# Two encoder layers on one core: products of the merge gates move one stage ahead, and the recurrence works in strips of 32 keys

## The chip, the cores and the metric

The kernel runs on one core of one Trainium2 chip. The metric is the device time of one execution in microseconds; of several runs the median is taken.

## The reference

A batch of one sequence of 512 tokens with 1024 features goes through two layers, in fp32. `w_in` (1024 features in, 8608 out) is one projection whose output is cut into the inputs of three mixers and three gates; each mixer's output is projected, weighted by the sigmoid of its gate and summed:

```python
for l in range(DEPTH):                                  # DEPTH = 2
    h = _rmsnorm(x, g_mix[l])
    (a_cq, a_ckv, a_kr, b_q, b_ff, b_fb, b_i, b_g,
     c_q, c_k, c_v, gate_a, gate_b, gate_c) = _split_cols(h @ w_in[l], IN_SPLITS)
    y_a = _mla(a_cq, a_ckv, a_kr, ...)                   # latent attention
    y_b = _hgrn2(b_q, b_ff, b_fb, b_i, b_g, ...)         # gated linear recurrence, both directions
    y_c = _window_gqa(c_q, c_k, c_v, ...)                # windowed attention
    merged = (jax.nn.sigmoid(gate_a) * (y_a @ w_br_a[l])
              + jax.nn.sigmoid(gate_b) * (y_b @ w_br_b[l])
              + jax.nn.sigmoid(gate_c) * (y_c @ w_br_c[l]))
    x = x + merged @ w_out[l]
    x = x + _cross(_rmsnorm(x, g_x[l]), _rmsnorm(mem, g_mem[l]), ...)
    x = x + _swiglu(_rmsnorm(x, g_ffn[l]), ...)
return _rmsnorm(x, g_final)
```

The recurrence has 8 heads with keys of 128 and values of 64 features. For each of its two directions a state `S_t = diag(f_t) S_(t-1) + k_t v_t^T` is read by `q_t`; the reference computes it in chunks of 16 tokens. Since `f` only decays, the sum over both directions can be written as one matrix of scores over all 512 x 512 pairs of tokens, times the values.

## The kernel before

Activations lie feature by feature: a tile has 128 features (or tokens of keys) on its partitions and the 512 tokens along its free axis. A product on TensorE takes a weight block of 128x128 (or smaller) and moves up to 512 columns through it into a bank of PSUM; there are eight banks, handed out in turn.

**Weights.** Every weight is streamed from DRAM in units of four blocks (256 KB, tile `wraw`), in the order in which the program asks for them. `_next` (by way of `_fetch`, L112) keeps the fetches up to five units ahead, on SP's queue. `_part` makes two tiles of a unit, up to three units ahead: `whi` is the value rounded to fp32r (ScalarE, L120), `wlo` what the rounding left (VectorE, L121). With activations split the same way (`split`, L180 on ScalarE, L181 on VectorE), `mm3` makes one fp32-like block product of three fp32r products. A projection of 1024 features into 128 is eight blocks, two units, 24 products. All matmuls are issued from one line, L151.

**Order.** The text of the program gives what each engine is to do; a scheduler may take instructions of one engine in another order where nothing forbids it, and each engine then runs its own list in order. Bars to free reordering are the rotating buffers: 25 tiles of 256 KB (`t2`), 14 large ones (`c8`), the eight banks, five units of weights.

**Stages of a layer.** Recurrence (`hgrn`), latent attention (`mla`), windowed attention (`window`), then output projection, cross attention and feed-forward part. `fillers` is a list of pieces of other work; `fill` takes the next piece at marked places of the attention stages. In the kernel before, `branch` makes these pieces: for two columns of blocks at a time it issues two gate projections, their sigmoids (L519), and two output projections of the mixer, each multiplied by its gate and added into `merged`. The pieces of mixer B fill the `mla` stage, those of A the `window` stage, those of C, but for a first gate, come behind it.

**Recurrence.** For each head `take_z` makes sigmoids of the two forget projections (L307, L308) and `hgrn_decay` (L394 on), for each direction, makes log decays, scans them (L411), and writes queries and keys scaled by decays: `qk` (tile `c`, keys at L439) for the pairs inside a strip of 32 tokens, and `lf`, `lr` (tile `c`, L457, on POOL and VectorE) for pairs of strips at four distances. `hgrn_scores` (L460 on) then makes the matrix of scores of a head. For each of four groups `j` of 128 tokens it takes `bd` and `bb`, the full 128x128 squares of both directions, of which only the four 32x32 blocks on the diagonal are kept by a mask (L482); neighbouring strips and halves are separate products of 32x32 and 64x64 that write over their parts of `bd`. Pairs of tokens in different groups are eight wide products into three further banks `g`. The result is split (L487, L488, and `split`) into `ah` and `al`; `vturn` turns the values so that keys lie on partitions, and splits them too. The value product of a head is twelve fp32r products into one bank, half of whose rows are that head's and are copied out (L369).

The loop over heads `i` is written so that scores of head `i`, projections of head `i + 2` (`take_z`, `take_q`), the value product of head `i` and the decay of head `i + 2` follow each other; every second head (odd `i`) adds a gate of the recurrence itself (`g`), a sum over features and the normed output `y`.

Of the kernel before, what the change touches and what calls it, by code (L numbers as in the profile page):

```python
# [48 lines left out]
def _consts():  # L49
# [21 lines left out]
    mb = same & (p[:, None] >= p[None, :])  # L71
# [4 lines left out]
class _K:  # L76
# [119 lines left out]
    def setup(self):  # L196
# [25 lines left out]
        self.zz = self.tl("zz", [P, 2, 4, P])  # L222
        nc.gpsimd.memset(self.zz, 0.0)
# [66 lines left out]
    def hgrn(self, l, x, xg, acc):  # L290
# [13 lines left out]
        def take_z(hd, zs):  # L304
# [27 lines left out]
        take_z(heads[1], [proj("f", 1), proj("b", 1)])  # L332
# [3 lines left out]
        a = self.hgrn_scores(heads[0])  # L336
        decay(heads[1])
        y = self.pairs4(4)
        for i in range(8):
            pr = i // 2  # L340
            if i > 0:
                a = self.hgrn_scores(heads[i])
            if i % 2 == 0:
                osb = self.t2()
                if 0 < i < 6:
                    values(pr + 1)
            else:
# [6 lines left out]
            if i < 6:  # L354
                take_z(heads[i + 2], [proj("f", i + 2), proj("b", i + 2)])
# [7 lines left out]
            ob = self.bank()  # L363
            vh, vl = vs[pr]
# [95 lines left out]
    def hgrn_scores(self, hd):  # L460
# [5 lines left out]
        bd, bb = self.bank([P, 4, P]), self.bank([P, 4, P])  # L466
# [12 lines left out]
        ah, al = self.c8([P, 4 * T], F32R), self.c8([P, 4 * T], F32R)  # L479
        z = self.zz  # L480
        for i, b in enumerate((bd, bb)):
            nc.vector.copy_predicated(z[:, i], self.msk[:, i].unsqueeze(1).to_broadcast([P, 4, P]), b)  # L482
        zd = self.t2(shape=(P, 4, P))
        tt(zd, z[:, 0], z[:, 1], op=ALU.add)
        dg = lambda a: bass.AP(a.tensor, a.offset, [list(a.ap[0]), [640, 4], [1, P]])
        dh, dl = dg(ah), dg(al)
        nc.scalar.activation(dh, zd, AF.Copy)  # L487
        tt(dl, zd, dh.bitcast(F32), op=ALU.subtract)  # L488
        h0, h1 = slice(0, P), slice(P, 2 * P)
        for i in range(3):  # L490
# [12 lines left out]
            s = slice(i * 640 + 128, (i + 1) * 640)  # L503
            self.split(ah[:, s], al[:, s], g)
        return ah, al

    def branch(self, l, gate, wname, rows, y, h, merged, first):

        nc = self.nc
        allr = np.arange(D)  # L510
        st = {}

        def gates(c):
# [648 lines left out]
```

## Time and profile before

| | |
|---|---|
| median of 3 runs | 2450.2 us (2447.57 to 2451.07) |
| profiled execution, its own time | 2445.72 us |
| its span, first to last instruction | 2443.9 us |
| mean granted clock of TensorE | 0.994 |
| TensorE matmuls | 2396.9 us, 98% |
| VectorE | 1503.9 us, 62% |
| ScalarE | 1194.2 us, 49% |
| GpSimd | 262.9 us, 11% |
| DMA, mean | 90 GB/s, 29.8% of 16 engines |

The share of an engine is its busy time over the span; matmuls overlap, so a busy TensorE need not be at its peak. The granted clock is a share of 2.4 GHz: 1.00 is 2.4 GHz, 0.50 is 1.2 GHz. The list of waits says on what an engine that stood idle was waiting, and its sum is time lost only on the engine that sets the end. In windows each engine is given as busy time and the number of instructions under way in that stretch.

### The profile page before, as it was taken

The numbers are of one execution on the slowest core, as the hardware profiler recorded it, in microseconds if no ns is written. First come the engines' busy times: TensorE is split into PE (matmuls) and PEld (weight loads), VectorE is DVE, ScalarE is ACT, GpSimd is POOL, SyncE is SP. The second block draws the span as 40 slices with busy tenths as digits, with TensorE's granted clock in tenths as the row PEclk, the third lists the DMA queues.
The fourth block names the chain that finished last, engine by engine and source line by source line (L and its number), as shares of the span: only waits on it lengthen the run. The fifth ranks groups of instructions, "written<-read, shape, count | busy, mean of one in ns | idle before, by whom it ended". The sixth has DMA issues, their size and how long they took to land.

```text
span 2443.9 us, 32499 instructions
## 1 busy us (share of the span) xinstructions
PE 2396.9 (98%) x11974; PEld 1966.2 (80%) x11974; DVE 1503.9 (62%) x2745; ACT 1194.2 (49%) x2169; POOL 262.9 (11%) x197
## 2 busy tenths in 40 slices
PE   8999999999999999999998999999999999999998
PEld 6788877788888888888877887877888888888886
DVE  8877766665565655355577786666656566553553
ACT  7666665555444533233466665654544444332332
POOL 2455300000000000000035452000000000000000
PEclk9999999999999999999999999999999999999999
DMA  4212222123442333333421212212324522333332
GB/s 141 61 57 70 82 70 66 62 82 107 151 139 86 91 96 95 99 95 99 127 77 61 70 61 74 74 57 71 90 84 148 147 87 82 96 95 99 96 98 75
DMA packets 119681, 220.96 MB, mean 90 GB/s; under 512 B 13281, under 2 KB 15585, under 8 KB 119137
## 3 DMA queue, kind: packets, MB, share of 16 engines
q1 hardware_dynamic: 119520, 218.88, 29.8%
q8 instruction: 94, 1.54, 0.3%
q14 instruction: 67, 0.54, 0.1%
HBM read 214.63 MB, written 4.19 MB: 90 GB/s over the span
## 4 chain that ended last, share of the span: by engine, by line
PE 85%; DVE 8%; ACT 3%; POOL 2%; issue 1%; DMA 1%; SPq 0%; DVEq 0%; ACTq 0%; POOLq 0%
PE ps L151 83%; POOL t L404 2%; DVE c L457 1%; PE ps L643 1%; DVE smx L411 1%; PE ps L784 1%; POOL t L408 1%; DVE c L439 1%; DVE t L411 1%; DVE wlo L121 1%; DVE c L181 0%; ACT whi L120 0%; DVE c L438 0%; DVE zz L482 0%; DMA c<-in_memT_dram 0%
## 5 line engine op out<-in xcount | busy, mean ns | idle before, releaser
L151 PE MATMUL ps<-c,whi 128*128 128x512 f32 (+1 forms) x5696 | 1734.7, 387 | 6.5 <-ACT whi L120 6.2
L151 PEld LDWEIGHTS ps<-c,whi 128*128 128x128 f32 x5696 | 1059.4, 188 | 232.8 <-issue 10.4
L151 PE MATMUL ps<-c,wlo 128*128 128x512 f32 (+1 forms) x2848 | 1098.4, 386 | 15.3 <-DVE wlo L121 15.2
L120 ACT ACTIVATE whi<-wraw 128x512 fp32r<-128x512 f32 x764 | 475.3, 630 | 858.1 <-PE ps L151 626.3
L121 DVE TENSOR_TENSOR wlo<-wraw,whi 128x512 fp32r<-128x512 f32 x764 | 521.0, 690 | 552.9 <-ACT whi L120 539.8
L151 PEld LDWEIGHTS ps<-c,wlo 128*128 128x128 f32 x2848 | 536.1, 188 | 127.3 <-DVE wlo L121 20.5
L151 PE MATMUL ps<-c,t 128*128 128x512 f32 (+6 forms) x1024 | 188.0, 393 | 4.0 <-DVE c L181 3.7
L404 POOL TENSOR_SCALAR t<-t 128x512 f32<-128x512 f32 x32 | 71.8, 2244 | 1067.4 <-ACT t L401 1065.9
L151 PEld LDWEIGHTS ps<-c,t 128*128 128x128 f32 (+2 forms) x1024 | 127.8, 176 | 48.0 <-issue 20.2
L457 POOL TENSOR_TENSOR c<-c,smx 128x256 f32<-128x256 f32 x128 | 144.9, 1161 | 73.8 <-DVE c L438 61.4
L982 DVE TENSOR_TENSOR t<-ps,t 128x512 f32<-128x512 f32 x112 | 76.3, 688 | 103.0 <-PE ps L151 103.0
L151 PE MATMUL ps<-c 128*32 128x32 f32 (+3 forms) x1280 | 110.6, 259 | 5.5 <-DVE c L439 5.5
L151 PEld LDWEIGHTS ps<-c 128*32 128x32 f32 (+2 forms) x1280 | 96.8, 151 | 21.9 <-DVE c L439 4.0
L181 DVE TENSOR_TENSOR c<-ps,c 128x512 fp32r<-128x512 f32 (+2 forms) x126 | 80.2, 650 | 23.7 <-ACT c L180 23.4
L180 ACT ACTIVATE c<-ps 128x512 fp32r<-128x512 f32 (+2 forms) x126 | 68.4, 565 | 43.9 <-PE ps L151 42.6
L964 DVE TENSOR_TENSOR c<-ps,c 128x512 f32<-128x512 f32 x64 | 44.2, 691 | 72.8 <-PE ps L151 72.8
L457 DVE TENSOR_TENSOR c<-c,smx 128x256 f32<-128x256 f32 x128 | 67.7, 587 | 0.3
L408 POOL TENSOR_TENSOR t<-t,t 128x512 f32<-128x512 f32 x32 | 45.1, 1409 | 86.7 <-ACT t L407 86.7
L181 DVE TENSOR_TENSOR c<-t,c 128x512 fp32r<-128x512 f32 (+1 forms) x84 | 51.9, 632 | 2.9 <-ACT c L180 2.9
L180 ACT ACTIVATE c<-t 128x512 fp32r<-128x512 f32 (+1 forms) x84 | 48.0, 581 | 9.7 <-DVE t L390 3.3
L406 ACT ACTIVATE t<-t 128x512 f32<-128x512 f32 x32 | 20.1, 630 | 62.5 <-POOL t L404 62.5
L411 DVE TENSOR_TENSOR_SCAN t<-cst,t 128x512 f32<-128x512 f32 x32 | 40.8, 1275 | 15.8 <-POOL t L408 15.8
(145 smaller groups left out, 1830.6 us busy)
## 6 DMA issues: line engine op xcount, KB each, us to landing
wraw<-in_w_dram SPq DMA_DIRECT2D x764, 256.0 KB, 2.6
c<-in_xT_dram SPq DMA_DIRECT2D x16, 256.0 KB, 5.2
t<-in_bias_dram SPq DMA_DIRECT2D x16, 192.0 KB, 3.0
c<-in_memT_dram SPq DMA_DIRECT2D x3, 1024.0 KB, 8.1
xs<-c SPq DMA_DIRECT2D x8, 256.0 KB, 2.4
c<-xs SPq DMA_DIRECT2D x8, 256.0 KB, 5.3
out_dram<-t SPq DMA_DIRECT2D x8, 256.0 KB, 2.1
t<-in_rope_dram SPq DMA_DIRECT2D x4, 256.0 KB, 3.4
```

Source lines behind the costliest of these rows:

```text
L120: self.nc.scalar.activation(hi, raw, AF.Copy)
L121: self.nc.vector.tensor_tensor(lo, raw, hi.bitcast(F32), op=ALU.subtract)
L151: self.nc.tensor.matmul(o, a, b, start=start, stop=stop)
L180: nc.scalar.activation(hi, src, AF.Copy)
L181: nc.vector.tensor_tensor(lo, src, hi.bitcast(F32), op=ALU.subtract)
L404: nc.gpsimd.tensor_scalar(g, f, TINY, KNEE, op0=ALU.max, op1=ALU.min)
L408: nc.gpsimd.tensor_tensor(f, f, g, op=ALU.add)
L411: scan = lambda o, m, x: nc.vector.tensor_tensor_scan(o, m, x, 0.0, op0=ALU.mult, op1=ALU.add)
L439: nc.vector.scalar_tensor_tensor(ki, kk, omlb, cc, op0=ALU.mult, op1=ALU.mult)
L457: eng.tensor_tensor(ov, sv, ev, op=ALU.mult)
L964: nc.vector.tensor_tensor(x[c], b, xold[c], op=ALU.add)
L982: self.nc.vector.tensor_tensor(t, b, r, op=ALU.mult)
```

## The change

Three things change.

**Scores in strips.** For each group `j` the full squares are replaced by products of strips: four 32x32 on the diagonal of the forward direction (`bd`), four of the backward one (`bb`, now 32 columns wide), four of neighbouring strips, and four of 32 keys by 64 queries for the halves. Each sits on the 32 rows of PSUM of its strip. The wide products stay. The scores `a` are kept in one fp32 tile, not split in two: the predicated copies take the mask, ScalarE copies (`dg` and the three banks `g`), and four additions on 32 partitions bring in `bb`.

**Values of two heads at once.** `vturn` leaves the values in fp32. In odd iterations eight fp32 products, alternating between the two heads' halves of the rows, make the output of both heads in one bank, which is copied out once.

**Gates one stage ahead.** The gate projections of B are issued in the recurrence (two ahead of head 1's projections, then one in each of iterations 0 to 5), those of A in the `mla` stage, six of C in the `window` stage and two behind it. `gate_put` makes the sigmoid and writes it to DRAM; `out` reads it back ahead of its projection. The output projections stay where they were. This is 48 writes and 48 reads of 256 KB.

```diff
-        v = (self.t2(F32R, (P, 4, P)), self.t2(F32R, (P, 4, P)))
-        self.split(v[0], v[1], tb)
+        v = self.t2(shape=(P, 4, P))
+        nc.scalar.activation(v, tb, AF.Copy)
         return v
...
-        take_z(heads[1], [proj("f", 1), proj("b", 1)])
+        g0, g1, b0, b1 = self.projs("w_in", l, np.arange(D), [O_GB + ar, O_GB + P + ar, off["f"] + P + ar,
+                                                             off["b"] + P + ar], h)
+        take_z(heads[1], [b0, b1], [(0, g0), (1, g1)])
...
+            gs = [(i + 2, self.gate_proj(l, O_GB, i + 2, h))] if i < 6 else []
+            if i % 2 == 1:
                 g = proj("g", pr)
...
-                take_z(heads[i + 2], [proj("f", i + 2), proj("b", i + 2)])
+                take_z(heads[i + 2], [proj("f", i + 2), proj("b", i + 2)], gs)
...
-            for j in range(4):
-                s = slice(j * T, (j + 1) * T)
-                self.mm3(ob, (vh[:, j], vl[:, j]), (a[0][:, s], a[1][:, s]), j == 0, j == 3)
-            hf = slice(64 * (i % 2), 64 * (i % 2) + 64)
-            nc.scalar.activation(osb[hf], ob[hf], AF.Copy)
             if i % 2 == 1:
-                sq = self.t2()
+                ob = self.bank()
+                for j in range(4):
+                    for e in range(2):
+                        hf = slice(64 * e, 64 * e + 64)
+                        self.mm(ob[hf], vs[pr][:, j, hf], heads[i - 1 + e]["a"][:, j * T:(j + 1) * T], j == 0, j == 3)
+                osb, sq = self.t2(), self.t2()
+                nc.scalar.activation(osb, ob, AF.Copy)
...
-        for j in range(4):
-            js = slice(j * P, (j + 1) * P)
-            one(bd[:, j], qk[:, 1, js], qk[:, 0, js])
-            one(bb[:, j], qk[:, 3, js], qk[:, 2, js])
-        for j in range(4):
-            one(bd[0:64, j, 64:128], lf[:, 1, 1, 64 * j:64 * j + 64], lf[:, 1, 0, 64 * j:64 * j + 64])
-            one(bd[64:128, j, 0:64], lr[:, 1, 1, 64 * j:64 * j + 64], lr[:, 1, 0, 64 * j:64 * j + 64])
-            for i in range(2):
-                a, b = 64 * i, 64 * i + 32
-                ps = slice(64 * j + 32 * i, 64 * j + 32 * i + 32)
-                one(bd[a:a + 32, j, b:b + 32], lf[:, 0, 1, ps], lf[:, 0, 0, ps])
-                one(bd[b:b + 32, j, a:a + 32], lr[:, 0, 1, ps], lr[:, 0, 0, ps])
-        ah, al = self.c8([P, 4 * T], F32R), self.c8([P, 4 * T], F32R)
...
+        for j in range(4):
+            js = [slice(j * P + 32 * g, j * P + 32 * g + 32) for g in range(4)]
+            for g in range(4):
+                one(bd[q4[g], j, q4[g]], qk[:, 1, js[g]], qk[:, 0, js[g]])
+            for g in range(4):
+                one(bb[q4[g], j], qk[:, 3, js[g]], qk[:, 2, js[g]])
+            for g in range(4):
+                ps = slice(64 * j + 32 * (g // 2), 64 * j + 32 * (g // 2) + 32)
+                lt = lf if g % 2 == 0 else lr
+                one(bd[q4[g], j, q4[g ^ 1]], lt[:, 0, 1, ps], lt[:, 0, 0, ps])
+            for g in range(4):
+                ks = slice(64 * j + 32 * (g % 2), 64 * j + 32 * (g % 2) + 32)
+                lt = lf if g < 2 else lr
+                cs = slice(64, 128) if g < 2 else slice(0, 64)
+                one(bd[q4[g], j, cs], lt[:, 1, 1, ks], lt[:, 1, 0, 64 * j:64 * j + 64])
+        a = self.c8([P, 4 * T])
+        nc.vector.copy_predicated(self.zz, self.msk[:, 0].unsqueeze(1).to_broadcast([P, 4, P]), bd)
+        nc.vector.copy_predicated(self.zb, self.msk[:, 1, 0:32].unsqueeze(1).to_broadcast([P, 4, 32]), bb)
...
+        nc.scalar.activation(dg, self.zz, AF.Copy)
+        for g in range(4):
+            tt(dg[q4[g], :, q4[g]], self.zz[q4[g], :, q4[g]], self.zb[q4[g]], op=ALU.add)
...
-            self.split(ah[:, s], al[:, s], g)
-        return ah, al
+            nc.scalar.activation(a[:, i * 640 + 128:(i + 1) * 640], g, AF.Copy)
+        hd["a"] = a
...
+    def gate_put(self, sd, c, b):
+        sg = self.t2()
+        last = self.nc.scalar.activation(sg, b, AF.Sigmoid)
+        self.nc.sync.dma_start(sd[:, c], sg)
+        return last
...
+            def run():
+                sg = self.t2()
+                nc.sync.dma_start(sg, sd[:, c])
+                pb = self.projs(wname, l, rows, [c * P + np.arange(P)], y)[0]
...
-            self.fillers += self.branch(l, O_GB, "w_br_b", np.arange(512), yb, h, merged, True)
+            br = self.branch(l, sd, "w_br_b", np.arange(512), yb, merged, True)
+            sd, gs = self.gates(l, O_GA, h)
+            for c in range(0, KC, 2):
+                self.fillers += gs[c:c + 2] + [both(br[c], br[c + 1])]
...
-            self.fillers += self.branch(l, O_GA, "w_br_a", np.arange(512), ya, h, merged, False)
+            br = self.branch(l, sd, "w_br_a", np.arange(512), ya, merged, False)
+            sd, gs = self.gates(l, O_GC, h)
+            for c in range(6):
+                self.fillers += [gs[c], br[c]]
+            self.fillers += br[6:]
```

The mask `mb` becomes the triangle of a 32-wide strip, and `zz`, `zb` are the buffers that the predicated copies fill. The function `vtoken` of `mla` goes, since `vturn` now does the same.

On TensorE, at the scores of head 0 of layer 1, the kernel before had (`c_77` is `qk`, `c_81` is `lf`, `c_85` is `lr`, `ps_594` is `bd`, `ps_595` is `bb`):

```order
L151 MATMUL ps_594<-c_77_361 128x128
L151 MATMUL ps_595<-c_77_361 128x128
L151 MATMUL ps_594<-c_81_384 64x64
L151 MATMUL ps_594<-c_85_415 64x64
L151 MATMUL ps_594<-c_81_384 32x32
L151 MATMUL ps_594<-c_85_415 32x32
```

In the kernel after, the same place has (`ps_673` is `bd`, `ps_674` is `bb`):

```order
L151 MATMUL ps_673<-c_77_362 32x32 x4
L151 MATMUL ps_674<-c_77_362 32x32 x4
L151 MATMUL ps_673<-c_81_385 32x32
L151 MATMUL ps_673<-c_85_416 32x32
L151 MATMUL ps_673<-c_81_385 32x32
L151 MATMUL ps_673<-c_85_416 32x32
L151 MATMUL ps_673<-c_81_385 32x64 x2
L151 MATMUL ps_673<-c_85_416 32x64 x2
L151 MATMUL ps_673<-c_77_362 32x32 x4
```

Before, the pair of 128x128 came four times ahead of the small shapes; then one pair of 64x64 and two pairs of 32x32 followed for each j. Now a j has sixteen products of 32 output rows, and the next j follows with the same shape.

SP's queue, from the projections ahead of head 1 to the end of iteration 0, had only weight units before:

```order
L112 DMA wraw_557<-in_w_dram 128x512
L112 DMA wraw_575<-in_w_dram 128x512
L112 DMA wraw_720<-in_w_dram 128x512
L112 DMA wraw_738<-in_w_dram 128x512
L112 DMA wraw_757<-in_w_dram 128x512
```

Now the writes of two gates stand among them, and one more in each iteration:

```order
L112 DMA wraw_607<-in_w_dram 128x512
L112 DMA wraw_636<-in_w_dram 128x512
L536 DMA gate_b<-t_114_573 128x512
L536 DMA gate_b<-t_115_576 128x512
L112 DMA wraw_654<-in_w_dram 128x512
L112 DMA wraw_827<-in_w_dram 128x512
```

The units that follow in the list are issued behind the write, which waits for ScalarE's sigmoid `t_114` or `t_115`.

On ScalarE, in the window stage of layer 1, the split of the second query (L183) stood behind two weight units, with the sigmoids of a pair of gates (L519) ahead of them:

```order
L519 ACTIVATE t_951_4585<-ps_4546 128x512
L787 ACTIVATE c_952_4587<-ps_4588 128x256
L787 ACTIVATE c_952_4587<-ps_4597 128x384
L120 ACTIVATE whi_4667<-wraw_4625 128x512
L120 ACTIVATE whi_4800<-wraw_4644 128x512
L183 ACTIVATE t_977_4704<-ps_4606 128x512
```

Now it is (L535 is the sigmoid of a gate, L793 the copy that was L787):

```order
L120 ACTIVATE whi_5305<-wraw_5143 128x512
L120 ACTIVATE whi_5323<-wraw_5282 128x512
L535 ACTIVATE t_1016_5164<-ps_5124 128x512
L793 ACTIVATE c_1017_5167<-ps_5168 128x256
L793 ACTIVATE c_1017_5167<-ps_5177 128x384
L183 ACTIVATE t_1022_5186<-ps_5087 128x512
```

The split moved right behind a gate's sigmoid and the two copies; `ps_5124`, the gate's projection, comes on TensorE after the query's own, `ps_5087`.

## Rows read from the trace of the kernel before

**Rows 1.** The page, busy time, share of the span and instructions of each engine.

```profile
PE 2396.9 (98%) x11974; PEld 1966.2 (80%) x11974; DVE 1503.9 (62%) x2745; ACT 1194.2 (49%) x2169; POOL 262.9 (11%) x197
```

**Rows 2.** Windows of the recurrence: length, busy (PE, PEld, DVE, ACT, POOL), clock, DMA.

```profile
85.00:120.00 35.00, 30.92 (x182) 24.95 (x181) 30.64 (x55) 23.48 (x40) 17.55 (x16) 0.95 0.16 49
120.00:152.00 32.00, 30.78 (x185) 25.14 (x184) 24.29 (x48) 19.63 (x35) 19.44 (x12) 1.00 0.22 64
152.00:185.00 33.00, 32.97 (x199) 27.30 (x198) 26.59 (x49) 21.70 (x38) 13.36 (x12) 1.00 0.20 66
```

**Rows 3.** Waits of TensorE, 50 to 1540 us: total, times, longest.

```profile
PE ps L151 <- DVE wlo L121: 15.2, 10, 3.7
PE ps L151 <- DVE c L439: 5.5, 2, 3.8
PE ps L151 <- DVE c L181: 3.7, 2, 1.9
```

**Rows 4.** Windows of the stretches at half clock, the long one and one of three.

```profile
56.88:67.12 10.24, 9.46 (x72) 8.06 (x73) 9.37 (x15) 4.81 (x9) 4.51 (x5) 0.50 0.39 122
...
1326.64:1330.05 3.41, 3.41 (x9) 2.65 (x8) 3.41 (x7) 3.38 (x6) 0.00 (x0) 0.50 0.27 62
```

**Rows 5.** Timeline of TensorE in layer 1: start, length, line, shape, count, idle before.

```profile
57.66 10.56 PE L151 MATMUL ps<-c 128*128 128x128 f32 x78 [3.78 <-DVE c L439]
67.98 0.70 PE L151 MATMUL ps<-c,whi 128*128 128x512 f32 x2
...
78.99 2.88 PE L151 MATMUL ps<-c,t 128*128 128x512 f32 x12
81.71 0.62 PE L151 MATMUL ps<-c,whi 128*128 128x512 f32 x2
```

**Rows 6.** Windows of one head's scores (iteration 0), then of single groups of products.

```profile
125.62:127.40 1.78, 1.78 (x17) 1.75 (x15) 0.81 (x2) 1.47 (x3) 0.16 (x1) 1.00 0.69 169
127.40:129.35 1.95, 1.95 (x50) 1.42 (x48) 0.81 (x1) 0.00 (x0) 1.87 (x2) 1.00 0.36 118
129.35:132.00 2.65, 2.65 (x25) 2.44 (x17) 0.91 (x4) 0.50 (x1) 2.12 (x1) 1.00 0.00 0
...
127.76:127.82 0.05, 0.05 (x8) 0.05 (x8) 0.00 (x0) 0.00 (x0) 0.05 (x1) 1.00 0.59 232
127.82:127.96 0.15, 0.15 (x10) 0.10 (x9) 0.00 (x0) 0.00 (x0) 0.15 (x1) 1.00 1.03 393
127.96:128.43 0.46, 0.46 (x20) 0.35 (x13) 0.00 (x0) 0.00 (x0) 0.46 (x1) 1.00 0.45 169
```

**Rows 7.** Groups of TensorE by form, 120 to 185 us: busy, mean ns, idle before.

```profile
L151 PE MATMUL ps<-c,wlo 128*128 128x512 f32 x65 | 25.4, 391 | 1.2 <-DVE wlo L121 1.2
...
L151 PE MATMUL ps<-c 128*32 128x32 f32 x64 | 2.1, 206 | 0.0
```

**Rows 8.** Timeline of TensorE, values in the latent attention.

```profile
414.54 3.65 PE L151 MATMUL ps<-c,t 128*64 128x512 f32 x16
```

**Rows 9.** Groups of VectorE by form, 120 to 185 us.

```profile
L181 DVE TENSOR_TENSOR c<-ps,c 128x512 fp32r<-128x512 f32 x6 | 3.8, 677 | 0.0
...
L488 DVE TENSOR_TENSOR c<-t,c 128x512 fp32r<-128x512 f32 x2 | 1.8, 883 | 0.0
...
L425 DVE TENSOR_TENSOR smx<-smx,t 128x64 f32<-128x64 f32 x4 | 1.1, 268 | 0.0
```

**Rows 10.** Timeline of all engines in the window stage of layer 1.

```profile
495.59 1.25 PE L784 MATMUL ps<-cst,t 128*128 128x128 f32 x10
...
496.15 0.58 ACT L519 ACTIVATE t<-ps 128x512 f32<-128x512 f32 x1
...
496.60 0.71 PE L151 MATMUL ps<-c,whi 128*128 128x512 f32 x2
496.63 0.76 ACT L787 ACTIVATE c<-ps 128x256 f32<-128x256 f32 x2
```

**Rows 11.** The page, DMA issues: count, KB each, median us to landing.

```profile
c<-xs SPq DMA_DIRECT2D x8, 256.0 KB, 5.3
```

**Rows 12.** Window of the scores of head 0 in layer 2, behind a wait.

```profile
1296.00:1299.55 3.55, 3.55 (x62) 3.03 (x62) 2.88 (x4) 3.51 (x6) 2.60 (x4) 1.00 0.00 0
```

More of the change, by code (lines that the diff above doesn't have):

```diff
@@ L70, in _consts @@
     mf = (~same) | (p[:, None] <= p[None, :])
-    mb = same & (p[:, None] >= p[None, :])
+    mb = (p[:, None] % 32) >= p[None, :]
     m = np.concatenate([mf, mb], 1).astype(np.int32)
@@ L302, in take_q, with take_z @@
             nc.scalar.activation(hd["q"], b, AF.Copy)
-        def take_z(hd, zs):
+        def take_z(hd, zs, gs=()):
+            for c, b in gs:
+                self.gate_put(sd, c, b)
             for d, z in enumerate(zs):
@@ L335, in hgrn @@
         values(1)
-        a = self.hgrn_scores(heads[0])
+        self.hgrn_scores(heads[0])
         decay(heads[1])
@@ L479, in hgrn_scores @@
-        ah, al = self.c8([P, 4 * T], F32R), self.c8([P, 4 * T], F32R)
[L480 to L488, printed above, removed]
+            js = [slice(j * P + 32 * g, j * P + 32 * g + 32) for g in range(4)]
@@ L502, in hgrn_scores, with gates, chunk @@
                 one(g[:, 384:512], lr[:, 2, 1, h1], lr[:, 2, 0, h1])
-            s = slice(i * 640 + 128, (i + 1) * 640)
-            self.split(ah[:, s], al[:, s], g)
-        return ah, al
[L507 to L513, printed above, removed]
+            nc.scalar.activation(a[:, i * 640 + 128:(i + 1) * 640], g, AF.Copy)
+        hd["a"] = a
+    def gates(self, l, gate, h):
+        sd = self.dr.tile([P, KC, T], F32, name=f"gate{l}_{gate}")
+        st = []
+        def chunk(c):
             def run():
-                st[c] = self.projs("w_in", l, allr, [gate + c * P + np.arange(P)], h)[0]
+                st.append(self.gate_proj(l, gate, c, h))
                 if c % 2 == 1:
                     for i in (c - 1, c):
-                        sg = self.t2()
-                        last = nc.scalar.activation(sg, st[i], AF.Sigmoid)
-                        st[i] = sg
+                        last = self.gate_put(sd, i, st.pop(0))
                     if c == KC - 1 and gate == O_GC:
@@ L523, in gates, with gate_proj, branch, out @@
             return run
-        def out(c0):
-            def run():
-                for c in (c0, c0 + 1):
-                    sg = st.pop(c)
-                    pb = self.projs(wname, l, rows, [c * P + np.arange(P)], y)[0]
-                    if first:
-                        nc.vector.tensor_tensor(merged[c], pb, sg, op=ALU.mult)
-                    else:
-                        nc.vector.tensor_tensor(sg, pb, sg, op=ALU.mult)
-                        nc.vector.tensor_tensor(merged[c], merged[c], sg, op=ALU.add)
-            return run
-        res = []
-        for c in range(0, KC, 2):
-            res += [gates(c), gates(c + 1), out(c)]
-        return res
+        return sd, [chunk(c) for c in range(KC)]
+    def gate_proj(self, l, gate, c, h):
+        return self.projs("w_in", l, np.arange(D), [gate + c * P + np.arange(P)], h)[0]
+    def gate_put(self, sd, c, b):
[3 more added lines that the diff above has]
+        return last
+    def branch(self, l, sd, wname, rows, y, merged, first):
+        nc = self.nc
+        def out(c):
+            def run():
+                sg = self.t2()
+                nc.sync.dma_start(sg, sd[:, c])
+                pb = self.projs(wname, l, rows, [c * P + np.arange(P)], y)[0]
+                if first:
+                    nc.vector.tensor_tensor(merged[c], pb, sg, op=ALU.mult)
+                else:
+                    nc.vector.tensor_tensor(sg, pb, sg, op=ALU.mult)
+                    nc.vector.tensor_tensor(merged[c], merged[c], sg, op=ALU.add)
+            return run
+        return [out(c) for c in range(KC)]
     def mla_pre(self, l, h):
@@ L672, in mla @@
         self.fill()
-        v = vtoken(vf)
+        v = self.vturn(vf)
         cq = self.mst["n", "cq"]
@@ L1087, in layers, with both @@
         assert self.pos == UNIT and self.unit == NUNIT - 1, (self.unit, self.pos, len(self.rec))
+def both(f, g):
+    def run():
+        f()
+        g()
+    return run
 def _t5_bucket(rel):
```

33 lines of the change are left out of this document (12 added, 21 removed).

## The prediction

> **What bounds the kernel now.** I read the page first: TensorE is busy for 98% of the span, VectorE for 62%, ScalarE for 49% [rows 1]. So time can come from three sources: TensorE work that gets shorter, TensorE's waits, and stretches at the lower of its clock's two levels. The windows by stage come next [rows 2]. From 120 us on, the recurrence runs in pairs of heads of 65 us (120:152 and 152:185); TensorE is busy for 63.8 of them, VectorE for 24.29 + 26.59 = 50.9 and ScalarE for 41.3. Its start is looser: of the 35 us of 85:120 TensorE is busy for 30.9 and VectorE for 30.6, at a granted clock of 0.95. The list of waits shows what TensorE lacks [rows 3]: the scores of head 0 wait for `c` of L439, 5.5 us in the two layers; products wait for low halves of weights (`wlo`, L121), 15.2 us in ten times, and of scores (`c` of L181), 3.7 us. The clock falls to 0.50, which is 1.2 of its 2.4 GHz, for 10.24 us once and for 3.41 us three times in this stage, each time beside one of those waits [rows 4].
>
> **What a product costs.** An fp32 product runs as two passes, an fp32r product as one. The twelve fp32r value products of a head take 2.72 us (78.99 to 81.71) [rows 5], so 0.227 each, and a projection of 24 of them 5.44. The scores of one head take 6.38 us, and the windows cut them in three [rows 6]: eight full squares 1.78 us, 24 small products 1.95, wide products 2.65. Only the first two change: 3.73 us a head.
>
> **The change, part by part.**
>
> *Strips.* 32 products (64 passes) become 64 of 32 keys each (128 passes), in groups of four that sit on the four column strips of the array. The trace has such a group, the four 32x32 products behind each pair of 64x64. The finest windows start at its first pass [rows 6]: 0.05 us from the first quad of passes to the second, then 0.15 until the next shape begins. Of this 0.15 the pass itself is 0.05, and some 0.1 is the change of tile shape. In the new order three groups of 32x32 and one of 32x64 follow each other for each j without such a change. I take 2 x 0.05 for a group of 32 columns, and 2 x 0.08 for one of 64, between 0.05 and the 1.78/16 = 0.11 of a full pass. That is 4 x (3 x 0.10 + 0.16) = 1.84, with the change of shape at both ends 2.0 us. Below, if only the columns count and groups overlap: a full pass of 128 columns is 0.11, so 32 columns are 0.028, and 24 x 0.028 + 8 x 0.056 + 0.1 = 1.2. Above, by busy time [rows 7]: 2.1 us for the eight groups of two heads are 0.26 a group; less the change of shape, 0.08 for each of its quads, and with 0.11 where 64 columns move 24 x 0.08 + 8 x 0.11 = 2.8. I take 2.0, since 0.05 is read from the very operation. Saved: 3.73 - 2.0 = 1.7 us a head, 16 heads: **-27 us** (from -15 to -40).
>
> *Values.* Twelve fp32r products a head, 5.44 us for a pair, become eight fp32 products for both heads at once, each with weights 64 columns wide, one half of the array a head. The trace has this form among the values of the MLA stage: sixteen passes 128*64 with 512 columns in 3.65 us [rows 8]. So 5.44 - 3.65 = 1.8 for each of eight pairs: **-14 us**. As the form is the same the bounds are close, -12 to -15.
>
> *Waits at the front, and the clock.* Two gate projections now stand ahead of head 1's: 10.9 us of TensorE work between the first decay and the scores that wait for it. Both waits for `c` of L439 (3.8 and 1.7) are shorter than this and go. The two long waits for low halves (3.7 and about 2.3; the other eight of the ten are near 1.15 each, 15.2 - 9.2 = 6.0) and those for L181 (3.7 in all) [rows 3] come from VectorE being full at the start, 30.6 of 35 us [rows 2]. VectorE loses per head three L181 of 0.68 and L488 of 0.88, a sum (L484) of the same size and two thirds of a predicated copy, put at 0.68 and 0.5, and gets four adds on 32 partitions, 0.27 each by the nearest row (L425) [rows 9]: about 3 us less. Per pair the low half of `v` goes too, 0.7. The gate of each iteration brings two L121, 1.4 us. A pair then has 50.9 - 6 - 0.7 + 2.8 = 47 us of VectorE beside 65 - 3.4 - 1.8 + 10.9 = 70.7 of TensorE: 66% instead of 78%. So I let all four go: 5.5 + 6.0 + 3.7 = 15. With them go the halved stretches: scores from 57.66 last until 67.98, 10.3 us instead of 6.4 [rows 5, 6], so 3.9; three stretches of 3.41 us [rows 4] cost half, 5.1. Together **-15 and -9 us** (from 0 to -24).
>
> *What comes up instead.* In even iterations TensorE waits 1.2 us for a low half, in 120:185 as in the others [rows 7]. Up to there TensorE's work shrinks by about 1.7 us with the shorter strips and VectorE's by about 1.2 (one sum and most of a copy less ahead of that half); I add 0.6 each, six times: **+4** (0 to +7). In the window stage gate 1's projection is now the last one ahead of the second query's scores; TensorE has only ten transposes left behind it, 1.0 us (495.59 to 496.60) [rows 10]. On ScalarE the split of that query (L183) now stands behind this gate's sigmoid (0.58) and two copies (0.76) [rows 10], and is as long as the sigmoid; its low half on VectorE follows. That is 1.9 to 2.6 us against 1.0. I add 2 us a layer for this and the reads below: **+4** (0 to +6).
>
> *The gates themselves.* Their 48 projections move and cost TensorE the same; so do the 48 sigmoids on ScalarE. New are 48 writes and 48 reads of 256 KB on SP's queue; the nearest row is the reading back of `xs`, 5.3 us to land [rows 11]. The engines of the DMA are at a fifth of their time in this stage [rows 2]. Behind a write on SP wait the next weight units: the write waits for its sigmoid, and the fetches with it. Fetches run up to five units ahead, 5 x 2.72 = 13.6 us of products, less 5.3 to land and some 2 for the split, so a hold under 6 us costs nothing; a sigmoid follows its product by a few ScalarE instructions of 0.6. A read is asked for one projection of four blocks (2.72) or more ahead; where 5.3 us is not covered VectorE's multiply comes late, but TensorE only needs the bank back, and eight banks rotate. Hence nothing, at most +5. ScalarE gets two more table loads in iteration 0; it has some 45 of 70 us to do, which hides them.
>
> **Sum** against the profiled execution (2445.7 us): -27 - 14 - 15 - 9 + 4 + 4 = -57, so 2388.7. The median of the runs is 4.5 us higher, 2450.2, and I expect the same offset: **2393 us**.
>
> **Rivals.**
>
> *The strips bring nothing.* In the j-period of 0.46 us a 64x64 pair and a quad group have about half each [rows 6], 0.23 a group with its change of shape. If sixteen groups keep that price, the block is 3.7 us, as now, and the sum is -57 + 27 = -30: **2420**. For it speaks that nowhere in the trace two quad groups follow each other; against it that the second quad of a group already follows in 0.05. Chance 0.2.
>
> The Trainium skill ("TensorE: Matmul & The Clock Gate", "Wait — 56ns, not 53.3ns?") says that starts of small matmuls never come closer than some 25 ns; by it 128 passes are 3.2 us, 8 us are saved in all instead of 27, and the time is 2412. The trace disagrees within a burst: in the 0.05 us from 127.76 eight passes are under way [rows 6], and only the four of the 64x64 pair began before it, so four start within it.
>
> *The front stays as it is.* VectorE is still full at the start of a layer, the gates' weights add splits just there, and the waits and halved stretches remain: -57 + 24 = -33, **2417**. Against it: 10.9 us more cover and less VectorE work. Chance 0.1.
>
> *Slower: TensorE is bound by issue.* In a stretch right after a wait, which began with nothing queued on TensorE, 62 passes took 3.55 us [rows 12]: 57 ns each, whatever their size. At this price 128 passes are 7.3 us, 3.6 more a head, +57 in all against -30 for the rest: **2477**. It decides from 3.73 + 30/16 = 5.6 us a block, 44 ns a pass. The small products as they run now take 1.95/50 = 39 ns a pass, changes of shape included [rows 6]; that price would give 5.0 us, +20 - 30, and 2440. Chance 0.05: the 62 passes include full squares, whose columns alone explain much of it.
>
> **How the numbers follow.** Forecast 0.65, strips without effect 0.2, front as it is 0.1, slower 0.05. The low end is the forecast with the cheapest strips (-13) and few of the new stalls (-8), 2372, and some us below for both together with steady odd iterations: 2368. The high end takes in both middle rivals, 2420, and late reads: 2425. About 0.2%, 5 us, is what a measurement of this kernel can tell from no change; all cases but the last lie clear of it: faster 0.93, same 0.02, slower 0.05.
>
> **What would show it.** Strips: from the first 32x32 product to the first wide one 2.0 us (3.7 by the first rival, 7.3 by the last). Values: 3.65 us a pair. Front: no wait for the `c` of today's L439 in either layer, granted clock 1.00 in the recurrence. New: waits of 1.2 to 2.3 us in even iterations, one of about 2 us at the second query's split in each window stage. I am wrong if TensorE's busy time falls by less than 25 us, if waits for low halves add up to more than they do now, or if weights come late because a gate's write holds SP's queue.

## The result, and the profile of the changed kernel

The changed kernel takes 2417.4 us (2413.2 to 2419.0) against 2450.6 before in the same runs: a ratio of 0.9865, 95% interval 0.9848 to 0.9882, 33 us less. The forecast was 57 us less, 2393 us. The time lies inside the range, and the direction held; over 40% of the gain is missing, and one of the prediction's own signs of being wrong came true: waits for low halves add up to more than before.

The profiled execution (span 2417.2 us) is 26.7 us shorter than that of before. The page, line of busy times, beside [rows 1]:

```profile
PE 2352.1 (97%) x12934; PEld 1909.6 (79%) x12934; DVE 1467.4 (61%) x2721; ACT 1188.3 (49%) x2162; POOL 239.4 (10%) x197
```

TensorE does 45 us less, but its share of the span fell, so waits grew. The waits of TensorE, 50 to 1540 us, beside [rows 3] (total, times, longest):

```profile
PE ps L151 <- DVE wlo L121: 39.0, 14, 5.6
PE ps L151 <- DVE t L258: 1.5, 1, 1.5
PE ps L151 <- DVE smw L767: 1.4, 1, 1.4
PE ps L151 <- ACT t L183: 1.0, 1, 1.0
```

The waits for `c` of the first decay and of the scores' low halves are gone, as forecast. Those for low halves of weights went from 15.2 to 39.0 us. Windows of the changed kernel (length, busy of PE, PEld, DVE, ACT, POOL, clock, DMA), beside [rows 2, 4, 6, 8]:

```profile
85.00:120.00 35.00, 33.01 (x272) 26.93 (x270) 28.85 (x58) 23.71 (x42) 18.10 (x16) 1.00 0.27 84
132.60:134.02 1.42, 1.42 (x130) 1.32 (x129) 0.72 (x2) 1.29 (x3) 0.00 (x0) 1.00 0.12 30
134.02:136.66 2.64, 2.64 (x20) 2.44 (x17) 1.22 (x1) 0.00 (x0) 2.51 (x2) 1.00 0.31 101
154.50:161.33 6.83, 5.92 (x14) 4.68 (x15) 5.09 (x11) 4.72 (x8) 0.00 (x0) 0.50 0.57 179
...
122.50:126.08 3.58, 3.58 (x17) 1.06 (x16) 1.15 (x2) 2.26 (x4) 0.00 (x0) 1.00 0.86 276
...
132.60:208.12 75.52, 71.12 (x552) 56.18 (x551) 50.01 (x97) 44.15 (x77) 28.59 (x24) 0.95 0.25 78
```

First line: the start runs at full clock now (0.95 before), with TensorE busy for 33.0 of 35 us. Second and third: the strips of one head (head 2, as in [rows 6], whose iteration is 2 and not 0) take 1.42 us where squares and small products took 3.73, the wide products 2.64 as before. Fourth: 6.83 us at half clock, which begin within a wait and last beyond it. Fifth: the values of a pair take 3.58 us instead of 5.44. Last: a pair of heads, 75.5 us, with 71.1 of TensorE work, at a mean clock of 0.95.

Where a pair loses is its even iteration: one wait stands in each of iterations 2, 4 and 6 of a layer. The timeline of TensorE in iteration 4 (start, length, count, idle before and what ended it):

```profile
207.17 1.02 PE L151 MATMUL ps<-t,cst 128*128 128x512 f32 x2
208.12 4.30 PE L151 MATMUL ps<-c 128*32 128x32 f32 x144
...
231.75 0.80 PE L151 MATMUL ps<-c,wlo 128*128 128x512 f32 x1 [5.23 <-DVE wlo L121]
```

VectorE at the same time; L463 is what was L457, L496 the four small adds:

```profile
207.80 0.69 DVE L121 TENSOR_TENSOR wlo<-wraw,whi 128x512 fp32r<-128x512 f32 x1 [2.02 <-ACT whi L120]
...
210.88 1.23 DVE L417 TENSOR_TENSOR_SCAN t<-cst,t 128x512 f32<-128x512 f32 x1 [2.05 <-POOL t L414]
213.85 0.43 DVE L411 TENSOR_SCALAR t<-t 128x512 f32<-128x512 f32 x1 [1.75 <-POOL t L410]
...
220.35 2.56 DVE L463 TENSOR_TENSOR c<-c,smx 128x256 f32<-128x256 f32 x4
...
227.92 0.68 DVE L181 TENSOR_TENSOR c<-t,c 128x512 fp32r<-128x512 f32 x1
228.52 2.15 DVE L496 TENSOR_TENSOR c<-zz 32x128 f32<-32x128 f32 x4
230.71 3.40 DVE L121 TENSOR_TENSOR wlo<-wraw,whi 128x512 fp32r<-128x512 f32 x5
```

Between 208.5 and 230.7 VectorE runs a head's decay and makes no low half, and for 3.8 us of it waits for GpSimd, as it did before. TensorE has the scores and 62 products of units split before that, and is through at 226.5. In the kernel before the same place had 6.4 us of scores in front of the same 62 products:

```profile
190.76 6.62 PE L151 MATMUL ps<-c 128*128 128x128 f32 x80
...
212.59 0.50 PE L151 MATMUL ps<-c,wlo 128*128 128x512 f32 x1 [1.16 <-DVE wlo L121]
```

and this piece on VectorE:

```profile
202.82 0.74 DVE L482 COPY_PREDICATED zz<-msk,ps 128x512 f32<-128x512 int32 x1
203.46 1.42 DVE L457 TENSOR_TENSOR c<-c,smx 128x256 f32<-128x256 f32 x4
...
210.65 0.68 DVE L181 TENSOR_TENSOR c<-t,c 128x512 fp32r<-128x512 f32 x1
211.25 0.68 DVE L484 TENSOR_TENSOR t<-zz 128x512 f32<-128x512 f32 x1
211.86 0.68 DVE L121 TENSOR_TENSOR wlo<-wraw,whi 128x512 fp32r<-128x512 f32 x1
```

So the wait of 1.2 us became 5.2: 2.3 us because TensorE arrives earlier, 1.1 because the four L463 take 2.56 instead of 1.42, 1.5 because four adds (2.15) stand where one sum (0.68) stood, less 0.45 for the second masked copy; that makes 5.65 where 5.2 is measured. (Two small operations of the decay take 0.8 less and the low half itself 0.3 more, which closes the gap.) The window stage waits 2.5 us in layer 1 and 2.1 in layer 2, about half of it at L183, as forecast, and half for a softmax value, which was not.

### The profile page after: what moved, and what is told of

Its sections match the earlier page's. It is cut to its first block, busy times and chain, and to the rows that moved or that the text cites. A ratio compares the mean times of both kernels' runs of the same rounds, so it can differ in the third digit from the quotient of the medians.

```text
span 2417.2 us, 34636 instructions
## 1 busy us (share of the span) xinstructions
PE 2352.1 (97%) x12934; PEld 1909.6 (79%) x12934; DVE 1467.4 (61%) x2721; ACT 1188.3 (49%) x2162; POOL 239.4 (10%) x197
## 4 chain that ended last, share of the span: by engine, by line
PE 84%; DVE 8%; issue 4%; POOL 2%; ACT 2%; DMA 1%; SPq 0%; DVEq 0%; ACTq 0%; POOLq 0%
PE ps L151 81%; DVE c L463 2%; POOL t L410 1%; PE ps L658 1%; DVE wlo L121 1%; DVE smx L417 1%; PE ps L790 1%; DMA wraw<-in_w_dram 1%; DVE c L445 1%; POOL t L414 1%; DVE t L417 0%; ACT whi L120 0%; DVE c L444 0%; DVE c L181 0%; PE ps L939 0%
## 5 line engine op out<-in xcount | busy, mean ns | idle before, releaser
L151 PE MATMUL ps<-c,t 128*64 128x512 f32 (+6 forms) x960 | 167.5, 418 | 4.8 <-DVE smw L767 2.5
L151 PEld LDWEIGHTS ps<-c,t 128*64 128x64 f32 (+2 forms) x960 | 99.7, 167 | 55.6 <-issue 32.0
L463 POOL TENSOR_TENSOR c<-c,smx 128x256 f32<-128x256 f32 x128 | 118.4, 953 | 90.9 <-DVE c L444 60.9
L463 DVE TENSOR_TENSOR c<-c,smx 128x256 f32<-128x256 f32 x128 | 80.1, 683 | 0.1
L151 PEld LDWEIGHTS ps<-c 128*32 128x32 f32 (+1 forms) x2304 | 61.0, 120 | 11.8 <-PE ps L151 4.5
L151 PE MATMUL ps<-c 128*32 128x32 f32 (+3 forms) x2304 | 68.8, 218 | 0.0
L180 ACT ACTIVATE c<-ps 128x512 fp32r<-128x512 f32 (+2 forms) x78 | 42.7, 547 | 39.6 <-PE ps L151 38.6
L181 DVE TENSOR_TENSOR c<-ps,c 128x512 fp32r<-128x512 f32 (+2 forms) x78 | 49.3, 633 | 20.4 <-ACT c L180 20.0
```

The source lines that it names most:

```text
L151: self.nc.tensor.matmul(o, a, b, start=start, stop=stop)
L180: nc.scalar.activation(hi, src, AF.Copy)
L181: nc.vector.tensor_tensor(lo, src, hi.bitcast(F32), op=ALU.subtract)
L463: eng.tensor_tensor(ov, sv, ev, op=ALU.mult)
```

## The experiments

Theory A is that the low half is late because it stands behind a whole decay on VectorE, whose end TensorE now reaches sooner. Rival B blames the gates' own work there, rival C VectorE's speed; by the sum above C has a share, some 1.8 of the 4.1 us that the wait grew by in iteration 4. Ratios are to the kernel before, each with runs on the same chip.

**Log decays earlier (f1_logs).** The first part of `hgrn_decay`, up to the sum of logarithms, becomes a function of its own:

```diff
             if i < 6:
+                logs(heads[i + 2])
                 take_q(heads[i + 2], proj("q", i + 2))
```

> The changed kernel, with the part of a head's decay that makes log decays (scale, clamp, two logarithms, their sum) issued ahead of the head's query projection instead of behind it. In the changed kernel TensorE waits 4.4 to 5.6 us for a low half in each even iteration (30 us in six) and the clock is at half for 6.8 us behind each wait. Theory A: the low half is late because it stands on VectorE behind a whole decay, whose chain over ScalarE, GpSimd and VectorE starts only when the query projection is done; strips took 2.3 us of TensorE work from in front of it. By A the waits fall to under 1 us each and the half-clock stretches go: 24 to 30 us and about 20 us less, 2370 to 2385 us. Rival B: the gates' own splits, sigmoids and writes make the low half late: no change, 2417. Rival C: VectorE itself is too slow there (it shares time with GpSimd, and has four small adds of 0.3 to 0.5 us): waits stay above 2 us, 2395 to 2405.

2393.4 us, ratio 0.9779 (0.9756 to 0.9802): 24 us less than the changed kernel. The waits for low halves between 140 and 330 us, in the changed kernel and then in this one:

```profile
PE ps L151 <- DVE wlo L121: 14.9, 3, 5.2
```

```profile
PE ps L151 <- DVE wlo L121: 2.0, 5, 0.7
```

They and their half-clock stretches go, as A says; nothing of the gates was touched, against B. The scores of iteration 2 and the low half behind the decay, in the changed kernel and then in this one:

```profile
132.60 4.30 PE L151 MATMUL ps<-c 128*32 128x32 f32 x144
...
154.67 0.68 DVE L121 TENSOR_TENSOR wlo<-wraw,whi 128x512 fp32r<-128x512 f32 x1
```

```profile
138.19 4.30 PE L151 MATMUL ps<-c 128*32 128x32 f32 x144
...
155.72 0.68 DVE L121 TENSOR_TENSOR wlo<-wraw,whi 128x512 fp32r<-128x512 f32 x1
```

It is done 18.2 us behind the start of the scores instead of 22.8. One more low half now stands in the middle of the decay, but TensorE still runs 62 products between the scores and the late one, so it is the end of the decay that moved. The time is 8 us above A's span, since new waits of 5.3 and 5.2 us came at the start of each layer, where the edit also made both directions' logs of head 0 first.

**Squares again (e1_squares).** The full squares and the two full masked copies come back, with one add in place of four; the scores stay in one fp32 tile.

```diff
-            for g in range(4):
-                one(bd[q4[g], j, q4[g]], qk[:, 1, js[g]], qk[:, 0, js[g]])
...
+            one(bd[:, j], qk[:, 1, js], qk[:, 0, js])
+            one(bb[:, j], qk[:, 3, js], qk[:, 2, js])
...
+        tt(dg, self.z8[:, 0], self.z8[:, 1], op=ALU.add)
```

> The changed kernel with the scores' small blocks as they were before (full 128x128 squares, then 64x64 and 32x32 products), with two masked copies and one full add; values and gates as changed. The squares cost TensorE 2.3 us a head more than the strips by the two traces (6.37 against 4.06 us), 37 us in all. Theory A (TensorE's cover in front of the late low half is what strips took): waits in even iterations fall by 2.3 us each to 2 to 3 us, so 14 us come back and some of the 20 us of half clock: 2420 to 2440 us. Rival B (gates make it late): waits stay at 4.4 to 5.6, 2454. Rival C (VectorE's work): waits fall by the four adds alone, about 1.5 us, 2445.

2416.5 us, ratio 0.9875 (0.9849 to 0.9902): the same as with strips, though TensorE does 37 us more. Its waits between 140 and 330 us:

```profile
PE ps L151 <- DVE wlo L121: 5.2, 3, 2.9
```

They fell by 9.7 us in three, 3.2 each on average where A said 2.3 (the adds are gone as well, which C asks for), and five of six half-clock stretches went. Over both layers the six waits fell from 30.1 to 8.8 us, and half clock costs some 12 us less: 33 of the strips' 37 us are given back at these six places, and 4.4 more by short waits at the front (8.9 against 4.5).

**Gates in their old place (e2_gates_old).** The gate projections stand in the attention stages again, next to their use, and no gate goes through DRAM.

```diff
-            gs = [(i + 2, self.gate_proj(l, O_GB, i + 2, h))] if i < 6 else []
...
-            sd, gs = self.gates(l, O_GA, h)
-            for c in range(0, KC, 2):
-                self.fillers += gs[c:c + 2] + [both(br[c], br[c + 1])]
+            self.fillers += self.branch(l, O_GB, "w_br_b", np.arange(512), yb, h, merged, True)
```

> The changed kernel with the gates' products where they were before, one pair ahead of their use, and no gate in DRAM; strips and values as changed. Theory A: the waits in even iterations stay at 4 to 5 us with their half-clock stretches, and the front's waits (15 us) and half clock (9 us) come back in part: 2420 to 2440 us. Rival B: the even iterations' waits go back to 1.2 us (23 us less, and 20 of half clock), the front's come back (up to 24 us more): 2390 to 2400.

2452.5 us, ratio 1.0015 (1.0001 to 1.0029): strips and values alone gain nothing. Waits of its layer 1, 50 to 330 us:

```profile
PE ps L151 <- DVE wlo L121: 16.7, 5, 5.3
PE ps L151 <- DVE c L493: 5.3, 3, 2.4
PE ps L151 <- DVE c L442: 4.4, 2, 3.8
```

The waits of 5.3 us in iterations 4 and 6 are there without a gate, so B falls for these; that of iteration 2 is 2.8 us here in layer 1, where it was 4.4, and 4.4 in layer 2, as it was. The time is 13 us above A's span: besides the front's waits (`c` of L442, which was L439) the value products of the odd iterations now wait for the scores (`c` of L493, the adds), up to 2.4 us a pair. The changed kernel has no such wait, so the gate projections covered this too.

**The same order in the kernel before (c1_before_logs).** The edit of f1_logs on the kernel before.

> The kernel before, with the log decays ahead of the query projection as in the kernel f1_logs, nothing else. Theory A: its even iterations' waits of 1.2 us, 7 us in six, go: 2442 to 2447 us, at the edge of what is told from no change. Rivals B and C: no change.

2447.4 us, ratio 0.9999 (0.9989 to 1.0009): no change. Five of its six waits of 1.2 us stayed at 1.0 to 1.5, against A. In iteration 4 the low half is done 21.7 us behind the start of the scores, where it was 21.8. VectorE no longer waits for GpSimd there and is busy without a break from 194 to 214 us; but the second four multiplies take 2.69 us instead of 1.43, one low half more stands in between, and other operations took longer too. So earlier logs do not by themselves end a decay sooner; why they did by 4.5 us in f1_logs and not here is not shown. The time tells no more, since the edit brought the front waits of 5.0 to 5.7 us.

**Heads 0 and 1 in the old order (f2_logs_late).** As f1_logs, but the logs of these two heads stay in the decay.

```diff
                 for d in range(2):
+                    if hd["n"] < 2:
+                        self.hgrn_log(l, hd, d)
                     self.hgrn_decay(l, hd, d)
```

> As f1_logs, but the log decays stay where the changed kernel has them for heads 0 and 1. In f1_logs a wait of 5.2 to 5.3 us for a low half stands at the first decay of each layer, where the changed kernel waits 2.3 to 2.7 us (two waits), with 6.8 and 3.4 us of half clock. If that comes from making both directions' logs of head 0 first, these go back: 2 x 2.8 us of waiting and some 5 us of half clock less, 2380 to 2387 us. If the front is bound by VectorE in either order: no change, 2393.

2389.4 us, ratio 0.9754 (0.9738 to 0.9770). The waits of 5.3 and 5.2 us at the start of the layers went back to 1.9 and 2.6, each in two, but iteration 0 now waits 3.6 us (2.0 in the changed kernel), so less came than expected.

**Squares on top of it (e3_f2_squares).** f2_logs_late with the squares of e1_squares.

> As f2_logs_late with the squares of the kernel before in place of the strips. In the changed kernel squares instead of strips cost nothing (2416.5 against 2417.4 us). Theory A: the strips' 2.3 us a head were given back as waits and half clock; with the waits gone strips are worth their full 37 us, so this is 30 to 37 us slower than f2_logs_late: 2412 to 2422 us. Rival: strips are worth nothing whatever the waits: within 10 us of f2_logs_late.

2414.4 us, ratio 0.9855 (0.9840 to 0.9870), against 0.9754 with strips: strips are worth 25 us here, and 1 us, which is no more than the noise, in the changed kernel. That is below A's 30 to 37, in part since with squares the 3.6 us waits of iteration 0 (0.6 each) and a half-clock stretch behind one of them are gone as well, some 8 us.

**The window's pieces (f4_window).**

```diff
-            for c in range(6):
-                self.fillers += [gs[c], br[c]]
-            self.fillers += br[6:]
+            self.fillers += [gs[0], gs[1], br[0], gs[2], br[1], br[2], gs[3], gs[4], br[3], gs[5]] + br[4:]
```

> As f2_logs_late, with the window stage's pieces in an order in which an output projection of A, not a gate of C, stands between a query's projection and its scores. In the changed kernel the first such place waits 1.03 us for the query's split (L183) and 1.1 to 1.8 us for a softmax value, in each layer. If the gate's sigmoid ahead of the split is the cause, 4 to 5 us less than f2_logs_late; if the softmax itself is late, under 2 us.

2383.4 us, ratio 0.9729 (0.9715 to 0.9744), 6 us less than f2_logs_late; both waits are gone from the list. In its trace ScalarE makes the split with neither a sigmoid nor the two copies right ahead of it, which fits the first cause named; the run does not tell the sigmoid from the copies.

**More work for TensorE (e5_pad).** It adds products whose result is not used.

```diff
+            if i in (2, 4, 6):
+                pad = self.bank()
+                for n in range(12):
+                    self.mm(pad, h[0][0][:, 0:P], h[0][0], n == 0, n == 11)
```

> The changed kernel with twelve products (fp32r, 512 columns, 2.7 us) into a bank that nobody reads, right behind the scores of heads 2, 4 and 6 in both layers: 16 us more work for TensorE, ahead of the late low halves. Theory A (the low half comes at a time that VectorE's chain sets, TensorE only arrives early): the six waits of 4.4 to 5.6 us fall by 2.7 us each, so the added work costs nothing, and where the shorter wait no longer halves the clock for 6.8 us up to 3.4 us come back each: 2397 to 2417 us. If the low half waited for TensorE's progress (weight buffers, banks), the waits stay: 2417 + 16 = 2433 us.

2412.2 us, ratio 0.9842 (0.9826 to 0.9858): 16 us more work, and no more time than the changed kernel. Waits between 140 and 330 us:

```profile
PE ps L151 <- DVE wlo L121: 5.0, 2, 2.5
```

Two of the three fell by 2.74 us, just the work added: in iterations 4 and 6 the low half's time does not depend on TensorE. The third (4.4, iteration 2) fell to nothing: there the low half also came 1.7 us sooner, as VectorE's second four multiplies took 1.42 us instead of 2.68. Three half-clock stretches of 3.41 us are left of six of 6.83.

**Gates alone (e4_gates_only).** The kernel before with the gates' part of the diff and no other.

> The kernel before with the gates' products one stage ahead and in DRAM, scores and values as before. By the sums of the two traces the front's waits (15 us, less 6 that come new) and its half-clock stretches (9 us) are the gates' to bring, and about 4 us are lost in the window stage: theory, 2450 - 9 - 9 + 4 = 2432 to 2440 us. Rival: the gain of the changed kernel is all from the scores in one fp32 tile and the values (14 us and less VectorE work), and gates alone bring nothing: 2445 to 2455 us.

2439.9 us, ratio 0.9954 (0.9936 to 0.9971): 11 us less, as the sums of waits said. With e1_squares (0.9875) and the changed kernel (0.9865) the parts are, one on top of the other: gates 11 us, scores in one fp32 tile with values of two heads 19 us, strips 2 us, which is no more than the noise. In another order the parts differ: without the gates, strips and values gained nothing (e2_gates_old).

**Head 2 in the old order, too (f5_head3).**

> As f4_window, but head 2's decay also keeps the order of the changed kernel; log decays go ahead of the query projection from head 3 on. In f4_window a wait of 3.5 us with 3.4 us of half clock stands in iteration 0 of each layer, where the changed kernel waits 2.0 us. If that comes from the earlier logs of head 2: 1.5 us and 1.7 us of clock less in each layer, 2375 to 2381 us. Else no change, 2383.

2379.1 us, ratio 0.9703 (0.9689 to 0.9717), as expected: iteration 0 waits 2.0 us again, in two.

**A sixth unit of weights (e6_wb6).**

```diff
-NT2 = 25
-WB = 5
-LOOK = 3
+NT2 = 22
+WB = 6
+LOOK = 4
```

> The changed kernel with six buffers for weight units instead of five and units split four ahead instead of three; to make room, 22 instead of 25 tiles in the pool t2. Theory A: TensorE comes to each late low half after using up the five units that were split before the decay began; a sixth unit gives 2.7 us more work ahead of it, so the six waits of 4.4 to 5.6 us fall by 2.7 us each (16 us) and part of the half clock goes: 2385 to 2402 us. If the sixth unit's low half is also put behind the decay on VectorE, no change: 2417; if three tiles fewer hold work back, more than that.

2377.9 us, ratio 0.9708 (0.9686 to 0.9730): three numbers bring some 39 us, more than A's 15 to 32. Its waits, 50 to 1540 us:

```profile
PE ps L151 <- DVE wlo L121: 5.8, 4, 2.5
```

The two waits of layer 1's iterations 2 and 6 are gone, not just 2.7 us shorter, and that of iteration 4 is 2.4; with them go four of six half-clock stretches, and the short waits of the front fall from 8.9 to 0.9 us. TensorE reaches the wait of iteration 4 after 74 products, one unit of twelve more than the 62 of the changed kernel. That two waits vanish where 2.7 us were to come off, A's sum does not explain, and the run does not tell which of the three numbers did it.

**Both (f6_both).** f5_head3 with the three numbers of e6_wb6.

> f5_head3 and e6_wb6 together: log decays ahead of the query projection from head 3 on, the window's pieces in the other order, six buffers for weight units with 22 tiles in t2. e6_wb6 still waits 2.4 and 2.5 us in iteration 4 of each layer, with 3.4 us of half clock each, and 2 us in each window stage. Theory A: these go, some 5 + 3 + 4 us off 2378: 2364 to 2371 us. If three tiles fewer in t2 hold the earlier logs back, they take longer to come and it stays at 2375 to 2380.

2361.1 us, ratio 0.9633 (0.9605 to 0.9660), below A's span. All that TensorE waits for between 50 and 1540 us:

```profile
PE ps L151 <- DVE t L258: 3.0, 2, 1.5
PE ps L738 <- ACT t L735: 1.0, 1, 1.0
PE ps L151 <- DVE wlo L121: 0.9, 2, 0.6
```

This is the fastest version, 86 us (3.7%) below the kernel before and, by their medians, some 56 below the changed one.

## Why the prediction came out as it did

**Strips**: the mechanism was right and the term too small. The block is 1.42 us, not 2.0, near the low bound of 1.2. In the trace four passes of 32 columns begin 0.03 us behind the four ahead of them (132.69, 132.72, 132.75), and 0.06 where 64 columns move; the prediction took 0.05, read from the first two fours after a change of shape, which are 0.05 apart here too, and 0.08. So 2.3 us a head, -37 us instead of -27 on TensorE. The rivals on it (no effect, 57 ns a pass) were wrong on TensorE; the first nevertheless came out in the time (its 2420 to 2417 measured), by another way: the gain was given back as waiting. The rival of the unchanged front names 2417, the very time measured, and is wrong as well: the front did loosen, as the next part shows.

**Values**: 1.86 us a pair, -15 us; forecast -14.

**Front and clock**: mostly right. The long waits and all half-clock stretches of the start went; 8.9 us of short waits for low halves stand there where 17.4 us of all kinds stood. -8.5 and -9.6 us (half of the 19.3 us that products were busy at half clock) instead of -15 and -9. That all waits go was too much: those for low halves became short, 0.9 to 1.4 us, and stayed. VectorE's work of the pair in 132.60:208.12 fell to 50.0 us, not 47. The multiplies L463 make 2.1 of the 3 us; the eight adds take 0.28 us each there, as forecast, though four of them took 2.15 in iteration 4. VectorE by form, the kernel before in 120:185, then the changed one in that pair:

```profile
L457 DVE TENSOR_TENSOR c<-c,smx 128x256 f32<-128x256 f32 x16 | 8.5, 592 | 0.0
```

```profile
L463 DVE TENSOR_TENSOR c<-c,smx 128x256 f32<-128x256 f32 x16 | 10.6, 722 | 0.0
...
L496 DVE TENSOR_TENSOR c<-zz 32x128 f32<-32x128 f32 x8 | 2.2, 281 | 0.1
```

**Even iterations**: this is the step that failed. It said +0.6 us each, +4 in all. Measured are 30.1 us of waits where 7.1 stood, +23, and six stretches at half clock of 6.83 us. Products are busy for 3.3 to 5.9 us of a stretch, 26.9 in all, at half rate, so 13.4 us are lost. The first and the last of the six, and the sum:

```profile
154.50:161.33 6.83, 5.92 (x14) 0.50 0.57 179
...
1502.77:1509.60 6.83, 3.32 (x8) 0.50 0.30 97
sum 40.97, PE 26.89; mean PE 4.48
```

The step took 1.7 us less work for TensorE (2.3 measured) and let VectorE reach the low half 1.2 us sooner, for one sum and most of a copy less. It left the four adds out, which the prediction does count in VectorE's work of a pair: they came in front of the low half in iterations 4 and 6. And it took the multiplies L463 at their old time, where they run against GpSimd's and took 1.1 us longer. So in iteration 4 the low half came 1.8 us later behind the start of the scores, not 1.2 sooner. A 66% busy VectorE says nothing of when a low half is done in it. The step also did not see that a wait made longer than before brings the clock down with it, though [rows 4] show that beside each long wait. That the time stayed in the range is luck as far as this step goes: the room was made for two rivals that did not come about.

**Window stage**: +4.6 us, forecast +4, but only some 2 of it at the split that the forecast names; that a softmax value brought the rest is luck in the sum. **Gates in DRAM**: as forecast, nothing. Rows of the page on DMA issues, for two thirds of the gates:

```profile
gate<-t SPq DMA_DIRECT2D x32, 256.0 KB, 2.4
t<-gate SPq DMA_DIRECT2D x32, 256.0 KB, 4.0
```

Reads land in 4.0 us in the median, and TensorE waits for none.

Together -37 - 15 - 8.5 - 9.6 + 23 + 13.4 + 4.6 = -29 us, where 26.7 lie between the two profiled executions; the 2 us between them are not assigned. With the even iterations at +4 the sum would have been near -61.

## What to carry to other kernels

Work taken from the bottleneck engine is worth what the next arrival allows: where it waits for another engine a little (1.2 us here), that little grows by all that is saved in front of it. So look, at each place that waits already, at how far ahead the waited-for engine is, in units of buffers, before multiplying a gain by the number of places; here three numbers that set the buffering were worth more than the strips. Where a shorter job meets a fixed chain, mend the chain in the same change: start its head ahead of the work that need not come first, or keep one buffer more.

## What the runs showed of the hardware

Products of 128 by 32 on four column strips ran at 1.42 us for 128 passes, 11 ns a pass. The Trainium skill ("TensorE: Matmul & The Clock Gate", "Wait — 56ns, not 53.3ns?") gives some 25 ns as the least time between starts of small matmuls; by it the block would be 3.2 us, an estimate. For passes that sit on different column strips the trace disagrees.

The four multiplications L463 (L457 before) on VectorE, beside the four on GpSimd, mostly take one of two times: 1.42 us while GpSimd's take over 4.7, or 2.56 to 3.0 while these take 3.1 to 3.6. Both stand in the changed kernel's iteration 4, GpSimd's and VectorE's:

```profile
219.19 3.11 POOL L463 TENSOR_TENSOR c<-c,smx 128x256 f32<-128x256 f32 x4 [2.52 <-DVE c L444]
225.56 5.59 POOL L463 TENSOR_TENSOR c<-c,smx 128x256 f32<-128x256 f32 x4 [3.27 <-ACT whi L120]
```

```profile
226.58 1.42 DVE L463 TENSOR_TENSOR c<-c,smx 128x256 f32<-128x256 f32 x4
```

with 220.35 and 2.56 us (above) for the first. The Trainium skill ("SBUF — State Buffer", "🔬 SBUF: two separate sides") says that the two engines share a pair of ports which one instruction holds as a whole while the other engine's blocks; that one of the two is always slowed agrees with it. Which of them it is changed in this place with the order of work, and cost 1.1 us in iteration 4.

TensorE's clock fell to 0.50 within or soon behind all waits of 3.8 us and more in these traces outside the first microseconds of the program, as at 154.50 above, beside some of 1.8 to 3.7, as in [rows 4], and beside none of 1.5 us or less. With the long ones it mostly stayed there for 6.83 us, with the others for 3.41.
